# Another order of the opening, and other waits and stores in the last block, of a causal convolution with matrix taps

## Chip, cores and metric

The kernel runs on one core of a Trainium2 chip. The metric is the device time of one execution in microseconds (us); with several executions, the median. A profile of one execution shows what each engine did: PE (the matrix engine; PEld are its weight loads), DVE (vector), ACT (scalar), POOL (GpSimd) and SP, which here only issues transfers. TensorE's granted clock was 0.997 of full speed in the profiled execution.

## What is computed

```python
B, S, D, K = 8, 4096, 512, 8
for k in range(K):
    if k == 0:
        shifted = x
    else:
        shifted = np.concatenate([np.zeros((B, k, D)), x[:, :-k, :]], axis=1)
    out += np.matmul(shifted, kernel[k])
```

Each output row is a sum over eight taps: the row of x that lies k steps back, times a 512 x 512 matrix. x and the output are float32, 64 MiB each; the kernel multiplies in bf16 and adds in float32.

## The kernel before

**Tiling.** The 8 x 4096 rows are cut into 128 runs of 256 consecutive rows, and the 128 runs lie side by side: "row t" below is row t of all runs at once, a 128 x 512 tile. `XR` holds 20 such rows of x, transposed (channels on the partitions) and in bf16, as a ring; `place(t)` says where row t lies. A product (`product`, line 123) is four matmuls of 128 x 128 by 128 x 512 into one PSUM bank.

**The fast scheme.** Rows 0 to 3 (`HEAD`) are made directly, with 32 products (`direct`). The other 252 rows are made in 21 blocks of 12. A block has four nodes, PL, MI, H1 and H0, numbered 1 to 84. A node forms sums of rows on DVE (`node_z`, `node_A`, `node_s`, `node_F`, into the tiles `Z`, `S`, `F`), multiplies them with taps or with sums and differences of taps (the tiles W, made once by `wsum` and `plus` on DVE), nine products a node (eleven in the two leaf nodes, 3 and 4), and combines the results in PSUM and SBUF. So fewer products are needed than eight a row. The steps of a node, by the names in the order that is written out by hand: `a1`, `a0`, `u` (three products into a pair of banks `pp3`), `s0`, `s1` (ACT copies a seed from there into the banks of the lower and the upper output pair), `dt` (ACT copies the other bank to the tile `DT`), `v0`, `v1` (a product onto each seed), `d0`, `d1` (DVE makes the pair's other bank from it and `DT`), `l00` to `l11` (a product into each of the four banks), `e0`, `e1` (ACT or DVE takes each pair out to the tiles cc, dd, yy and stores it), `ga0` to `gb1` (`middle_half`, line 299: POOL adds the halves of the middle outputs of two tiles; when both halves are done SP stores the pair), and `ya0` (POOL subtracts one half of the lower output). The transposes `x12`, `x16`, `x20` bring the rows of the next block into `XR`, and `r0` to `r2` load rows three blocks ahead.

**What sets the order.** Nothing is scheduled by a planner: every engine works off its instructions in the order of the text, and waits on semaphores for its inputs. The opening (lines 430 to 643) is a list written out by hand; `go(k, name)` and `do(name, k)` in it run steps of the first nodes ahead of their block. From there `ORDER` (line 387) gives the sequence of a block, and `done` keeps what the opening has already run from running again. POOL issues all loads of x and of the taps (`load`, line 92), each of which turns float32 into bf16 on the way, and DRAM tiles (`xd`) hold rows of x until SP's transposes (`transpose`, line 98) move them to `XR`. SP issues the transposes and nearly all stores, one after the other. `behind` (line 111) makes a POOL instruction wait until the DVE operation issued last before it has ended. The tiles of outputs (`y`) are five, in turn.

**The last pair.** The last node is 84 (H0). Its upper output pair is written and stored by halves (lines 273 to 276), the lower half j = 0 on ACT's queue, then j = 1 on SP's. Both halves read the pair's banks in one tile (`pp1`), and the tile of dd that POOL reads in the last middle half, `ga1` of node 83.

Of the kernel before, what the change touches and what calls it, by code (L numbers as in the profile page):

```python
# [8 lines left out]
LO, HI, MID = 0, 1, 2  # L9
H1, H0, MI, PL = 0, 1, 2, 3  # L10
# [4 lines left out]
def kernel(  # L15
# [79 lines left out]
    def rows(o, t, n):  # L95
        return load(o, xr[:, t:t + n, :])
# [9 lines left out]
    def load_x(t):  # L106
        if t < RUN:
            xd[t] = dpool.tile([P, 4, D], bf, name="xd")
            return rows(xd[t], t, 4)

    def behind(i):
        tc.add_manual_dep(i.ins, last["dve"].ins.name,
                          mybir.DependencyInfo(mybir.DependencyClass.Sync, mybir.DependencyReason.DATA),
                          reason="behind")

    def transpose_x(t):
        if t < RUN:
            transpose(t, xd[t])
# [101 lines left out]
    def node_v(n, b_):  # L220
        if not n.leaf:
            product(n.p[b_][:, 1], comps(n)[2][1 + 2 * b_], W[n.a, b_, MID], False)

    def node_d(n, b_):
        if n.leaf:
            return
        p = n.p[b_]
        if b_ == LO:
            tt(p[:, 0], DT, p[:, 1], SUB)
        else:  # L230
            stt(p[:, 0], p[:, 1], -1.0, DT, SUB)
# [17 lines left out]
    def node_e(n, b_):  # L249
        p, t = n.p[b_], n.t + 2 * b_  # L250
        first = n.k <= 4
        if n.a == PL:
            cc[b_] = y_tile()
            if first:
                nc.scalar.mul(out=cc[b_], in_=p, mul=0.5)  # L255
            else:
                nc.scalar.copy(out=cc[b_], in_=p)  # L257
                dd[b_] = y_tile()
                nc.scalar.mul(out=dd[b_], in_=cc[b_], mul=-0.5)  # L259
        elif n.a == MI:  # L260
            if first:
                dd[b_] = y_tile()
                stt(dd[b_], p, -0.5, cc[b_], ADD)
            else:
                stt(dd[b_], p, 0.5, dd[b_], ADD)
        elif n.a == H1:
            yy[b_] = yy.get(b_) or y_tile()
            if first or b_ == HI:
                tt(yy[b_], p, dd[b_], ADD if first else SUB)
                store(t, yy.pop(b_))  # L270
            else:
                tt(yy[b_][:, 0], p[:, 0], dd[b_][:, 0], SUB)
        elif n.k == len(nodes) - 1 and b_ == HI:
            for j, eng in enumerate((nc.scalar, nc.sync)):
                stt(dd[b_][:, j], dd[b_][:, j], -1.0, p[:, j], SUB)
                eng.dma_start(out=orr[:, t + 8 + j, :], in_=dd[b_][:, j])
        else:
            if first:
                tt(dd[b_], dd[b_], p, SUB)
            else:  # L280
                stt(dd[b_], dd[b_], -1.0, p, SUB)
            store(t + 8, dd[b_])
# [14 lines left out]
        store(n.t + 4 + 2 * b_, cc[b_])  # L297

    def middle_half(n, b_, j):
        behind(nc.gpsimd.tensor_tensor(out=cc[b_][:, j], in0=cc[b_][:, j], in1=dd[b_][:, j], op=ADD))  # L300
        halves[b_] = halves.get(b_, 0) + 1
        if halves[b_] % 2 == 0:
            store(n.t + 4 + 2 * b_, cc[b_])

    halves = {}
# [1 line left out]
    def load_w(tap):  # L307
        n = K - 1 - tap
        load(W[n >> 2, n >> 1 & 1, n & 1], kr[:, :, tap, :])
# [10 lines left out]
    def wsum(a, b_, c_):  # L320
        p, m = terms(a, b_, c_)
        tt(W[a, b_, c_], p, m, SUB)
# [7 lines left out]
    def plus(*which):  # L330
        for b_, c_ in which:
            tt(W[PL, b_, c_], W[H0, b_, c_], W[H1, b_, c_], ADD)
# [7 lines left out]
    def transpose_pe(name, k, src, t0, t1):  # L340
        o = pair(k).bitcast(bf).rearrange("p a (b d) -> p (a b) d", b=2)
        for t in range(t0, t1):
            for c in range(DC):
                nc.tensor.transpose(o[:, t - t0, c * P:(c + 1) * P], src[:, t, c * P:(c + 1) * P],
                                    ident)
        bank[name] = o[:, 0:t1 - t0]
# [12 lines left out]
    def here(eng, t, name, a, b):  # L359
        eng(out=XR[:, place(t) + a:place(t) + b], in_=bank[name][:, a:b])  # L360

    def load_xin(t, a=0, b=4):
        rows(xin[t][:, a:b], t + a, b - a)
# [6 lines left out]
    def direct(tap, t):  # L370
        n = K - 1 - tap
        product(pd[t // 2][:, t % 2], XR[:, place(t - tap)], W[n >> 2, n >> 1 & 1, n & 1], tap == 0)
# [54 lines left out]
    def go(k, name):  # L427
        do("a1" if name == "b1" else name, k + AHEAD.get(name, 0))
# [30 lines left out]
    direct(1, 1)  # L459
    direct(1, 3)  # L460
    wsum(MI, HI, HI)
    direct(1, 0)
    load_w(5)
    plus((HI, HI))
    wsum(H1, HI, MID)
    direct(4, 1)
    load_w(3)
    plus((HI, LO))
    direct(5, 1)
    go(3, "d1")  # L470
    direct(4, 3)
    wsum(MI, HI, LO)
    direct(5, 3)
    wsum(H0, MID, LO)
    load_w(7)
    wsum(PL, HI, MID)
    direct(5, 2)
    wsum(MI, HI, MID)
    direct(3, 1)
    plus((LO, LO))  # L480
    wsum(PL, MID, LO)
    direct(3, 2)
    direct(3, 3)
    rows(H[:, 1:4], RUN - 7, 3)
    direct(7, 3)
    transpose_pe("h3", 2, H, 1, 4)
    direct(1, 2)
    load_w(6)
    wsum(MI, LO, LO)
    history(nc.scalar.copy, -7, "h3")  # L490
    direct(3, 0)
    wsum(H1, MID, LO)
    direct(7, 1)
    direct(6, 1)
    direct(7, 2)
    load_w(2)
    load_xin(4)
    load_xin(8, 0, 2)
    direct(6, 0)
    wsum(H1, MID, HI)  # L500
    go(3, "F0")
    wsum(H1, MID, MID)
    direct(7, 0)
    direct(5, 0)
    plus((LO, HI))
    wsum(PL, MID, HI)
    wsum(PL, LO, MID)
    go(2, "v1")
    wsum(MI, LO, HI)
    direct(2, 1)  # L510
    transpose_pe("x4", 3, xin[4], 0, 4)
    go(3, "d0")
    load_xin(8, 2, 4)
    direct(2, 0)
    here(nc.scalar.copy, 4, "x4", 2, 4)
    load_x(12)
    here(nc.scalar.copy, 4, "x4", 0, 2)
    transpose_x(12)
    wsum(PL, MID, MID)
    transpose_pe("x8", 2, xin[8], 0, 2)  # L520
    transpose_pe("x9", 2, xin[8], 2, 4)
    here(nc.scalar.copy, 8, "x8", 0, 2)
    wsum(MI, MID, HI)
    here(nc.scalar.copy, 10, "x9", 0, 2)
    load_x(16)
    fill(pair(3))
    z_rows(nodes[1], 0, 5)
    direct(6, 3)
    direct(2, 3)
    direct(6, 2)  # L530
    node_A(nodes[1])
    node_a1(nodes[1])
    direct(2, 2)
    go(3, "F1")
    z_rows(nodes[1], 5, 7)
    direct_out(0)
    s_rows(nodes[1], 0, 3)
    fill(pair(2))
    node_u(nodes[1])
    node_seed(nodes[1], 0)  # L540
    s_rows(nodes[1], 3, 5)
    node_seed(nodes[1], 1)
    node_a0(nodes[1])
    node_v(nodes[1], 0)
    node_dts(nodes[1])
    node_z(nodes[2])
    go(3, "v1")
    node_v(nodes[1], 1)
    node_F(nodes[1], 0)
    direct_out(1)  # L550
    node_A(nodes[2])
    wsum(MI, MID, LO)
    wsum(MI, MID, MID)
    node_d(nodes[1], 0)
    go(2, "v0")
    node_a1(nodes[2])
    for t in range(20, 52, 4):
        load_x(t)
    go(1, "l00")
    node_d(nodes[1], 1)  # L560
    go(1, "l01")
    go(1, "e0")
    go(1, "u")
    go(1, "F1")
    go(1, "s")
    go(1, "s0")
    go(1, "a0")
    go(1, "z")
    wsum(MI, LO, MID)
    go(1, "l11")  # L570
    go(1, "s1")
    go(1, "v1")
    go(4, "F1")
    go(1, "A")
    go(1, "l10")
    go(1, "dt")
    go(1, "e1")
    go(1, "d1")
    go(1, "a1")
    go(1, "v0")  # L580
    go(1, "F0")
    go(2, "a0")
    wsum(H1, LO, MID)
    go(1, "d0")
    go(2, "F1")
    go(2, "u")
    go(2, "l00")
    go(2, "s")
    wsum(H0, MID, HI)
    go(2, "l10")  # L590
    go(2, "l01")
    go(2, "s0")
    go(2, "e0")
    go(2, "dt")
    wsum(H0, MID, MID)
    go(2, "s1")
    go(2, "l11")
    go(2, "z")
    go(3, "s")
    go(2, "A")  # L600
    go(3, "l01")
    go(3, "l10")
    do("x12", 1)
    do("x16", 1)
    go(2, "e1")
    go(3, "g0")
    go(3, "dt")
    go(2, "a1")
    go(3, "z")
    go(3, "l00")  # L610
    go(3, "a0")
    go(3, "u")
    go(3, "l11")
    go(2, "d0")
    go(3, "e0")
    go(3, "A")
    go(3, "e1")
    go(3, "s0")
    do("x20", 1)
    go(2, "F0")  # L620
    go(4, "l01")
    go(4, "l00")
    go(3, "s1")
    go(4, "b1")
    go(4, "s")
    go(4, "F0")
    go(4, "l11")
    go(4, "a0")
    go(4, "e0")
    go(4, "u")  # L630
    go(4, "l10")
    go(4, "dt")
    go(4, "s1")
    go(4, "z")
    go(4, "A")
    go(4, "g1")
    go(4, "s0")
    go(4, "v0")
    go(4, "d0")
    go(4, "v1")  # L640
    go(4, "e1")
    go(4, "a1")
    go(4, "d1")

    done |= {(name, k) for name in ("ga0", "gb0", "ga1", "gb1", "x12", "x16", "x20")
# [41 lines left out]
```

## Time and profile before

| | |
|---|---|
| median of 3 runs (lowest to highest) | 719.75 us (719.42 to 720.0) |
| the profiled execution | 720.38 us, its span 718.6 us |
| granted clock of TensorE in it | 0.997 |
| bytes moved, mean rate | 138.87 MB by the queues, 193 GB/s |

Busy time by stretch of the profiled execution (us):

| stretch | PE | DVE | ACT | POOL |
|---|---|---|---|---|
| 0 to 10 | 7.05 | 1.16 | 4.25 | 6.67 |
| 10 to 20 | 8.50 | 2.53 | 1.85 | 2.45 |
| 20 to 30 | 10.00 | 9.67 | 0.54 | 2.14 |
| 30 to 40 | 9.57 | 9.54 | 2.27 | 2.57 |
| 40 to 50 | 7.27 | 9.93 | 5.05 | 1.03 |
| 50 to 60 | 9.26 | 9.43 | 4.67 | 0 |
| 60 to 100 | 39.83 | 38.20 | 14.92 | 0 |
| 100 to 700 | 597.45 | 595.05 | 251.37 | 147.73 |
| 700 to 710 | 10.00 | 7.51 | 2.69 | 3.81 |
| 710 to 718.6 | 0.40 | 1.29 | 0 | 1.26 |

How to read it: an engine that is busy for the whole of a stretch bounds it, one that has idle time there waits for another, and the view of idle times says for which. Matmuls overlap in the pipeline, so PE's busy time says when it had work, and the distance from one matmul's start to the next one's says how fast it went. In the lines of a timeline, the columns are the start, the time, the engine, the source line, the operation with its output and inputs, and in brackets the idle time before it with what ended it. All lines `L84` and `L87` are the helpers `tt` and `stt`, so the operations are told apart by their tiles.

### The profile page before, as it was taken

The page shows a single profiled execution, that of the slowest core. Times are in us where ns is not written, and L with a number is a line of the kernel's source. Part 1 is how long each engine was busy: PE and PEld are TensorE (multiplying, and loading weights), DVE is VectorE, ACT ScalarE, POOL GpSimd, SP SyncE. Part 2 cuts the span into 40 slices and gives each one's busy share as a digit, 9 for nine tenths or more (in the row PEclk, how much of TensorE's full clock was granted, in tenths as well). Part 3 has the DMA queues.
Part 4 walks back from the last instruction along what each step waited for, and adds up shares of the span by engine and source line. Part 5 has one row for each costly group of instructions (what it writes and reads, how often), then busy time and mean ns, then how long its engine had stood idle before and what let it go on. Part 6 is the DMA issues. An engine that isn't in the chain of part 4 may idle for free.

```text
span 718.6 us, 9022 instructions
## 1 busy us (share of the span) xinstructions
PE 699.3 (97%) x3270; PEld 314.9 (44%) x3270; DVE 684.3 (95%) x767; ACT 287.6 (40%) x448; POOL 167.6 (23%) x180
## 2 busy tenths in 40 slices
PE   7989999999999999999999999999999999999995
PEld 3444444444444444444444444444444444444442
DVE  2899999999999999999999999999999999999994
ACT  3043244443534434352443434354443435344341
POOL 4210013223041221304122130412213131221212
PEclk9999999999999999999999999999999999999998
DMA  9999559697797868868787887978787687756414
GB/s 193 209 212 226 181 119 257 147 234 179 206 211 183 247 155 231 185 190 205 192 247 151 236 179 208 220 179 235 165 237 173 205 224 177 225 127 192 150 59 176
DMA packets 159372, 138.87 MB, mean 193 GB/s; under 512 B 130144, under 2 KB 134240, under 8 KB 159200
## 3 DMA queue, kind: packets, MB, share of 16 engines
q1 hardware_dynamic: 145456, 99.89, 45.6%
q0 software_dynamic: 13728, 38.15, 31.2%
q8 instruction: 25, 0.41, 0.2%
q10 hardware_dynamic: 144, 0.26, 0.1%
q14 instruction: 19, 0.16, 0.1%
HBM read 77.33 MB, written 99.09 MB: 246 GB/s over the span
## 4 chain that ended last, share of the span: by engine, by line
PE 79%; DVE 10%; issue 2%; DMA 1%; POOL 1%; ACT 0%; POOLq 0%; DVEq 0%
PE pp L125 79%; DVE Z L84 4%; DVE S L84 1%; DVE y L87 1%; DMA out_dram<-y 1%; DVE F L84 1%; DVE w L84 1%; POOL y L300 1%; DVE y L84 1%; DVE pp L84 0%; DVE pp L87 0%; POOLq L682 0%; POOL xd L93 0%; ACT y L255 0%; ACT pp L212 0%
## 5 line engine op out<-in xcount | busy, mean ns | idle before, releaser
L125 PE MATMUL pp<-w,F 128*128 128x512 bf16 x1312 | 312.9, 379 | 1.0 <-DVE pp L87 0.7
L125 PE MATMUL pp<-w,Z 128*128 128x512 bf16 x960 | 233.9, 379 | 1.7 <-DVE Z L84 1.6
L300 POOL TENSOR_TENSOR y<-y 128x512 f32<-128x512 f32 x80 | 101.7, 1271 | 445.4 <-DVE F L84 327.7
L125 PEld LDWEIGHTS <-F 128*128 128x128 bf16 x1312 | 128.3, 98 | 156.6 <-issue 2.4
L125 PE MATMUL pp<-w,S 128*128 128x512 bf16 x672 | 158.8, 379 | 0.0
L84 DVE TENSOR_TENSOR Z<-XR 128x2048 bf16<-128x2048 bf16 (+3 forms) x109 | 154.7, 1438 | 2.4
L125 PEld LDWEIGHTS <-Z 128*128 128x128 bf16 x960 | 92.2, 98 | 118.7 <-DVE Z L84 10.3
L196 ACT COPY pp<-pp 128x512 f32<-128x512 f32 x82 | 46.7, 570 | 221.7 <-PE pp L125 221.7
L84 DVE TENSOR_TENSOR S<-Z 128x2560 bf16<-128x2560 bf16 (+1 forms) x81 | 114.7, 1416 | 0.0
L84 DVE TENSOR_TENSOR F<-S 128x1024 bf16<-128x1024 bf16 x160 | 111.4, 696 | 1.9 <-PE pp L125 1.9
L125 PEld LDWEIGHTS <-S 128*128 128x128 bf16 x672 | 65.7, 98 | 79.3
L212 ACT COPY pp<-pp 128x512 f32<-128x512 f32 (+1 forms) x84 | 48.8, 581 | 74.9 <-PE pp L125 74.9
L84 DVE TENSOR_TENSOR pp<-DT,pp 128x512 f32<-128x512 f32 x82 | 56.6, 690 | 1.3 <-PE pp L125 1.2
L87 DVE SCALAR_TENSOR_TENSOR pp<-pp,DT 128x512 f32<-128x512 f32 x82 | 56.8, 693 | 0.5 <-PE pp L125 0.5
L214 ACT ACTIVATE pp<-pp 128x512 f32<-128x512 f32 (+1 forms) x84 | 50.1, 597 | 14.3 <-PE pp L125 8.1
L84 DVE TENSOR_TENSOR Z<-Z 128x1024 bf16<-128x1024 bf16 x78 | 53.5, 686 | 0.7
L87 DVE SCALAR_TENSOR_TENSOR y<-pp,y 128x1024 f32<-128x1024 f32 x42 | 51.2, 1218 | 0.5 <-PE pp L125 0.5
L218 ACT COPY DT<-pp 128x512 f32<-128x512 f32 x82 | 48.9, 597 | 3.9 <-PE pp L125 3.9
L87 DVE SCALAR_TENSOR_TENSOR y<-y,pp 128x1024 f32<-128x1024 f32 (+1 forms) x41 | 48.4, 1184 | 1.7 <-POOL y L300 1.4
L257 ACT COPY y<-pp 128x1024 f32<-128x1024 f32 x40 | 40.7, 1016 | 22.9 <-PE pp L125 22.9
L93 POOL DMA_DIRECT2D xd<-in_x_dram x61 | 32.8, 537 | 65.2 <-DVE F L84 48.5
L259 ACT ACTIVATE y<-y 128x1024 f32<-128x1024 f32 x40 | 42.3, 1057 | 2.5 <-DMA out_dram<-y 0.4
(35 smaller groups left out, 248.9 us busy)
## 6 DMA issues: line engine op xcount, KB each, us to landing
out_dram<-y SPq DMA_DIRECT2D x127, 512.0 KB, 4.1
xd<-in_x_dram POOLq DMA_DIRECT2D x61, 512.0 KB, 5.3
w<-in_kernel_dram POOLq DMA_DIRECT2D x8, 512.0 KB, 17.0
w<-in_x_dram SPq DMA_DIRECT2D x1, 1024.0 KB, 4.8
w<-in_x_dram POOLq DMA_DIRECT2D x2, 512.0 KB, 13.7
XR<-xd SPq DMA_TRANSPOSE x61, 4.7
w<-in_x_dram POOLq DMA_DIRECT2D x2, 256.0 KB, 17.4
w<-in_x_dram POOLq DMA_DIRECT2D x1, 384.0 KB, 20.4
```

The costliest lines, as they stand in the source:

```text
L84: last["dve"] = nc.vector.tensor_tensor(out=o, in0=a, in1=b, op=op)
L87: last["dve"] = nc.vector.scalar_tensor_tensor(out=o, in0=a, scalar=by, in1=b, op0=MUL, op1=op)
L93: return nc.gpsimd.dma_start(out=o, in_=src)
L125: nc.tensor.matmul(bank, lhsT=comp[:, c * P:(c + 1) * P], rhs=w[:, c, :], start=start and c == 0, stop=c == DC - 1, skip_group_check=True)
L196: nc.scalar.copy(out=n.q[:, 0], in_=n.q[:, 1])
L212: nc.scalar.copy(out=o, in_=q)
L214: nc.scalar.mul(out=o, in_=q, mul=-1.0)
L218: nc.scalar.copy(out=DT, in_=n.q[:, 0])
L257: nc.scalar.copy(out=cc[b_], in_=p)
L259: nc.scalar.mul(out=dd[b_], in_=cc[b_], mul=-0.5)
L300: behind(nc.gpsimd.tensor_tensor(out=cc[b_][:, j], in0=cc[b_][:, j], in1=dd[b_][:, j], op=ADD))
```

## The change

Five things change; the products, sums and loads are the same ones as before.

1. The list of the opening from line 462 on stands in another order: the weight sums, the products of the direct rows, the PE transposes of rows 4 to 11 and the steps of nodes 1 to 8. `wsum(H1, HI, MID)`, `wsum(H1, MID, HI)` and `wsum(H1, MID, MID)` move back among the steps of the nodes; the transposes of rows 12 (`transpose_x(12)`) and 20 (`do("x16", 1)`) move behind the two direct outputs, the one of rows 16 (`do("x12", 1)`) behind that of rows 20.
2. The loads of rows 40, 44 and 48 move to the end of the opening's list, in the order 48, 40, 44, and wait for the DVE operation before them (`behind`).
3. In the last block, POOL's last half (`ga1` of node 83) is not held behind a DVE operation.
4. The two banks of the last node's upper pair lie in two tiles: the lower one moves to `pp3`, and node 84's `d1` writes it there.
5. The last middle output is stored by halves on ACT's queue, each when its half is done. The halves of the last upper pair are taken in the order upper, lower; the upper one is stored on ACT's queue and the lower one on SP's.

```diff
-    def behind(i):
+    def behind(i, k=0):
+        if k > len(nodes) - 5:
+            return
         tc.add_manual_dep(i.ins, last["dve"].ins.name,
...
+    class Apart:
+        def __init__(self, lo, hi):
+            self.banks = lo, hi
+
+        def __getitem__(self, i):
+            return self.banks[i[1]][:, i[1]]
+
     def node_d(n, b_):
         if n.leaf:
             return
+        if n.k == len(nodes) - 1 and b_ == HI:
+            n.p[b_] = Apart(pair(3), n.p[b_])
         p = n.p[b_]
...
         elif n.k == len(nodes) - 1 and b_ == HI:
-            for j, eng in enumerate((nc.scalar, nc.sync)):
+            for j, eng in ((HI, nc.scalar), (LO, nc.sync)):
                 stt(dd[b_][:, j], dd[b_][:, j], -1.0, p[:, j], SUB)
                 eng.dma_start(out=orr[:, t + 8 + j, :], in_=dd[b_][:, j])
...
     def middle_half(n, b_, j):
-        behind(nc.gpsimd.tensor_tensor(out=cc[b_][:, j], in0=cc[b_][:, j], in1=dd[b_][:, j], op=ADD))
+        behind(nc.gpsimd.tensor_tensor(out=cc[b_][:, j], in0=cc[b_][:, j], in1=dd[b_][:, j], op=ADD), b_ > j and n.k)
         halves[b_] = halves.get(b_, 0) + 1
-        if halves[b_] % 2 == 0:
+        if b_ and n.k > len(nodes) - 5:
+            nc.scalar.dma_start(out=orr[:, n.t + 6 + j, :], in_=cc[b_][:, j])
+        elif halves[b_] % 2 == 0:
             store(n.t + 4 + 2 * b_, cc[b_])
```

Of the opening's list, the new order of the parts that the prediction speaks of, with the rest left out:

```python
    wsum(MI, HI, HI)
    load_w(5)
    load_w(3)
    wsum(MI, HI, LO)
...
    plus((HI, LO))
    wsum(MI, HI, MID)
    go(3, "F1")
    plus((HI, HI))
    plus((LO, LO))
    wsum(PL, HI, MID)
...
    z_rows(nodes[1], 0, 5)
    node_A(nodes[1])
    load_x(12)
    transpose_pe("x9", 2, xin[8], 2, 4)
...
    for t in range(20, 40, 4):
        load_x(t)
...
    direct_out(1)
    go(1, "l01")
    go(1, "l00")
    node_d(nodes[1], 1)
    go(1, "e0")
    go(1, "u")
    go(1, "a0")
    transpose_x(12)
    go(1, "l10")
    go(1, "z")
    do("x16", 1)
...
    go(2, "e1")
    behind(load_x(48))
    go(3, "s")
...
    go(4, "l00")
    behind(load_x(40))
    go(4, "b1")
    go(4, "l10")
    behind(load_x(44))
```

More of the change, by code (lines that the diff above doesn't have):

```diff
@@ L461 @@
     wsum(MI, HI, HI)
+    load_w(5)
+    load_w(3)
+    wsum(MI, HI, LO)
     direct(1, 0)
-    load_w(5)
-    plus((HI, HI))
-    wsum(H1, HI, MID)
-    direct(4, 1)
-    load_w(3)
-    plus((HI, LO))
+    load_w(7)
+    direct(5, 3)
+    plus((HI, LO))
+    wsum(MI, HI, MID)
+    go(3, "F1")
+    plus((HI, HI))
+    plus((LO, LO))
+    wsum(PL, HI, MID)
+    rows(H[:, 1:4], RUN - 7, 3)
+    load_w(6)
+    direct(1, 2)
+    direct(4, 1)
+    wsum(H1, MID, LO)
+    direct(3, 0)
+    direct(4, 3)
@@ L469 @@
+    direct(3, 3)
+    load_w(2)
+    load_xin(4)
     direct(5, 1)
[L470 to L473, printed above, removed]
+    direct(3, 1)
     wsum(H0, MID, LO)
[L475 to L480, printed above, removed]
     wsum(PL, MID, LO)
-    direct(3, 2)
-    direct(3, 3)
-    rows(H[:, 1:4], RUN - 7, 3)
+    transpose_pe("h3", 2, H, 1, 4)
+    load_xin(8, 0, 2)
+    go(4, "F1")
     direct(7, 3)
-    transpose_pe("h3", 2, H, 1, 4)
@@ L487 @@
-    direct(1, 2)
-    load_w(6)
     wsum(MI, LO, LO)
     history(nc.scalar.copy, -7, "h3")
[L491 to L502, printed above, removed]
+    direct(6, 3)
+    wsum(H0, MID, HI)
+    plus((LO, HI))
+    direct(3, 2)
+    direct(6, 2)
+    direct(5, 2)
+    direct(5, 0)
+    direct(2, 1)
+    wsum(MI, LO, HI)
+    transpose_pe("x4", 3, xin[4], 0, 4)
@@ L503 @@
+    wsum(PL, MID, HI)
+    transpose_pe("x8", 2, xin[8], 0, 2)
     direct(7, 0)
-    direct(5, 0)
-    plus((LO, HI))
-    wsum(PL, MID, HI)
+    here(nc.scalar.copy, 4, "x4", 0, 2)
+    wsum(MI, LO, MID)
     wsum(PL, LO, MID)
[L508 to L512, printed above, removed]
+    wsum(MI, MID, HI)
     load_xin(8, 2, 4)
     direct(2, 0)
+    here(nc.scalar.copy, 8, "x8", 0, 2)
+    go(3, "d1")
+    wsum(PL, MID, MID)
+    direct(7, 1)
@@ L515 @@
     here(nc.scalar.copy, 4, "x4", 2, 4)
[L516 to L525, printed above, removed]
     fill(pair(3))
     z_rows(nodes[1], 0, 5)
-    direct(6, 3)
+    node_A(nodes[1])
+    load_x(12)
+    transpose_pe("x9", 2, xin[8], 2, 4)
     direct(2, 3)
-    direct(6, 2)
@@ L531 @@
-    node_A(nodes[1])
+    here(nc.scalar.copy, 10, "x9", 0, 2)
+    s_rows(nodes[1], 0, 3)
+    direct(6, 0)
+    z_rows(nodes[1], 5, 7)
     node_a1(nodes[1])
[L533 to L537, printed above, removed]
+    load_x(16)
+    wsum(H1, MID, HI)
+    s_rows(nodes[1], 3, 5)
+    direct(6, 1)
+    go(2, "v1")
     fill(pair(2))
     node_u(nodes[1])
+    node_z(nodes[2])
+    node_a0(nodes[1])
+    go(1, "F1")
+    node_A(nodes[2])
+    direct_out(0)
@@ L540 @@
+    node_dts(nodes[1])
+    direct(7, 2)
     node_seed(nodes[1], 0)
-    s_rows(nodes[1], 3, 5)
     node_seed(nodes[1], 1)
-    node_a0(nodes[1])
-    node_v(nodes[1], 0)
-    node_dts(nodes[1])
-    node_z(nodes[2])
-    go(3, "v1")
+    wsum(MI, MID, LO)
+    node_F(nodes[1], 0)
+    for t in range(20, 40, 4):
+        load_x(t)
+    direct(2, 2)
+    node_v(nodes[1], 0)
+    node_d(nodes[1], 0)
+    go(2, "F0")
+    wsum(MI, MID, MID)
+    node_a1(nodes[2])
+    go(1, "s")
     node_v(nodes[1], 1)
-    node_F(nodes[1], 0)
@@ L550 @@
     direct_out(1)
[L551 to L558, printed above, removed]
+    go(1, "l01")
     go(1, "l00")
     node_d(nodes[1], 1)
-    go(1, "l01")
     go(1, "e0")
     go(1, "u")
-    go(1, "F1")
-    go(1, "s")
-    go(1, "s0")
     go(1, "a0")
+    transpose_x(12)
+    go(1, "l10")
     go(1, "z")
-    wsum(MI, LO, MID)
+    do("x16", 1)
     go(1, "l11")
     go(1, "s1")
+    wsum(H1, MID, MID)
@@ L572 @@
+    go(1, "s0")
+    go(1, "v0")
+    go(1, "dt")
+    go(1, "F0")
+    go(1, "A")
+    go(1, "d0")
+    go(1, "a1")
+    go(2, "F1")
     go(1, "v1")
[L573 to L576, printed above, removed]
+    go(2, "l01")
+    go(2, "l00")
+    go(2, "a0")
+    go(2, "u")
     go(1, "e1")
     go(1, "d1")
[L579 to L589, printed above, removed]
@@ L590 @@
-    go(2, "l10")
-    go(2, "l01")
     go(2, "s0")
-    go(2, "e0")
     go(2, "dt")
     wsum(H0, MID, MID)
-    go(2, "s1")
+    go(3, "dt")
+    go(2, "s")
+    go(3, "v1")
+    go(2, "e0")
     go(2, "l11")
     go(2, "z")
-    go(3, "s")
+    do("x12", 1)
+    go(2, "l10")
+    go(3, "l00")
+    go(2, "s1")
+    go(2, "a1")
     go(2, "A")
     go(3, "l01")
-    go(3, "l10")
[L603 to L613, printed above, removed]
-    go(2, "d0")
[L615 to L620, printed above, removed]
+    go(3, "u")
+    go(2, "e1")
+    behind(load_x(48))
+    go(3, "s")
+    go(3, "z")
+    go(3, "l11")
+    go(3, "g0")
+    go(4, "g1")
+    wsum(H1, LO, MID)
+    go(3, "a0")
+    wsum(H1, HI, MID)
+    go(2, "v0")
+    go(3, "F0")
+    do("x20", 1)
+    go(3, "e0")
+    go(3, "s0")
+    go(3, "A")
+    go(3, "l10")
@@ L621 @@
+    go(3, "e1")
+    go(2, "d0")
     go(4, "l01")
+    go(3, "s1")
     go(4, "l00")
-    go(3, "s1")
+    behind(load_x(40))
     go(4, "b1")
+    go(4, "l10")
+    behind(load_x(44))
     go(4, "s")
+    go(4, "u")
+    go(4, "e0")
+    go(4, "s1")
+    go(4, "s0")
+    go(4, "l11")
+    go(4, "z")
     go(4, "F0")
-    go(4, "l11")
+    go(4, "A")
     go(4, "a0")
-    go(4, "e0")
-    go(4, "u")
-    go(4, "l10")
     go(4, "dt")
[L633 to L636, printed above, removed]
@@ L637 @@
-    go(4, "s0")
+    go(3, "d0")
+    go(4, "e1")
     go(4, "v0")
+    go(4, "v1")
+    go(4, "a1")
     go(4, "d0")
-    go(4, "v1")
-    go(4, "e1")
-    go(4, "a1")
     go(4, "d1")
```

## The prediction

> **What bounds the kernel now.** I read the page first (shares of the span), then a table of stretches, then the idle times of DVE and PE in the opening, and last the timeline, the issues and the DMA rate of the final 18 us.
>
> ```profile
> PE 699.3 (97%) x3270; PEld 314.9 (44%) x3270; DVE 684.3 (95%) x767; ACT 287.6 (40%) x448; POOL 167.6 (23%) x180
> ...
> 200.00:300.00 100.00, 100.00 (x464) 45.00 (x463) 99.14 (x112) 41.53 (x67) 26.05 (x27) 1.00 0.80 201
> ```
>
> The reader is to see two full engines: from 200 to 300 us PE is busy 100.00 of 100.00 us and DVE 99.14. A block of four nodes is 36 products of four matmuls, and the timeline has eight matmuls in 1.725 us (101.84 less 100.12), so PE needs 31.1 us a block; DVE has under 1% to spare beside it. Whatever the opening loses on either engine is therefore never caught up, and whatever it saves reaches the end. Only the opening and the last 10 us can be worth anything.
>
> ```profile
> 20.24 4.63 DVE L84 TENSOR_TENSOR w<-w,w 128x2048 bf16<-128x2048 bf16 x4 [2.62 <-DMA w<-in_kernel_dram]
> ...
> 31.07 1.40 DVE L84 TENSOR_TENSOR w<-w,w 128x2048 bf16<-128x2048 bf16 x1 [0.34 <-issue]
> ...
> 59.21 0.70 DVE L87 SCALAR_TENSOR_TENSOR pp<-pp,DT 128x512 f32<-128x512 f32 x1 [0.50 <-PE pp L125]
> ...
> 66.08 1.23 DVE L87 SCALAR_TENSOR_TENSOR y<-pp,y 128x1024 f32<-128x1024 f32 x1 [0.52 <-PE pp L125]
> ...
> 86.94 0.69 DVE L84 TENSOR_TENSOR pp<-DT,pp 128x512 f32<-128x512 f32 x1 [0.98 <-PE pp L125]
> ```
>
> These are DVE's waits in the opening, from the first weight sum (15.26) on: one for a tap's landing, one around the history copy, three for PE. The matmul rows show PE waiting in its turn: 1.62 us at 41.52, 1.21 at 49.38, 0.74 at 56.33.
>
> **The opening, reordered.** The two orders, read beside each other on DVE: from its first weight sum, 124 operations end at the same operation, and in both they are the same operations by shape and number; only their order differs. So their working time is the same, and I compare what lies between them. Back to back, the next one starts 0.08 us before the last ends (21.38 after a 20.24 start of 1.22); after an operation whose result it reads, it starts 0.035 us later (43.29 after 41.77 plus 1.48), so each such pair costs 0.12 us.
> Before: waits of 2.62, 0.55 (31.28 is where the cleared history row starts, 0.55 after DVE's last end), 0.50, 0.52 and 0.98, together 5.17 us; 17 short gaps, together 0.83; 22 lost overlaps of 0.08, 1.8. Sum 7.8 us.
> After, laid out with the durations of these rows (an operation starts when its engine is free and its last input is there, loads landing as before): one weight sum now stands ahead of the landing at 20.24 where two stood, so the wait grows to 20.24 - 16.48 = 3.76; four sums of 1.135 us later the next wanted pair, taps 3 and 7, lands at 25.32: 0.49. The clearing of the history row now comes at 32.1, when ACT's copy has been done for two us: nothing. The three waits for PE go: PE does the products that DVE wants first (the two seeds' products 0.4 to 0.7 us ahead near 60 us, the first outputs 1.2 to 1.7 us ahead at 64 to 67). The thinnest is at 86.5 us, where product and DVE meet within 0.02 us; if PE is late there, DVE loses that much. Nine dependent pairs remain, 0.3 us, and 11 lost overlaps, 0.9. Sum 5.5 us, so 2.3 us are saved. Laid out in the same way, the order of before brings DVE to its 125th operation at 141.9 us where the trace has 142.13; against that the saving is 2.0. I take 2.1.
> PE agrees: its gaps after 15 us (0.5, 1.8, 1.3, 0.9 and some 1.8 in small ones up to 120) become 0.5, 0.2, 1.95 (at 41.4, for node 1's sums), 0.6, 0.2 and 0.7. That is about 2 us as well. Bounds: 2.3 above; below, if the thin places slip by half a us each and the extra waits at two semaphores (0.09 instead of 0.035 us) show in all pairs, 0.7.
>
> **Loads and transposes.** The loads of rows 40, 44 and 48 leave the opening's queue and are tied to DVE operations near 68, 79 and 80 us. Cost nothing: their transposes come at 126 us and later, a steady load takes 5.3 us, so 40 us cover them; POOL has nothing else before 104.5 us. The software queue then ends with rows 36, whose load lands at 55.4 instead of 63.4 us. Rows 12's transpose is issued behind the two direct stores, at 53.0 instead of 39.81:
>
> ```profile
> 39.81 20.49 SPq L100 DMA_TRANSPOSE XR<-xd  x1
> 60.36 1.21 SPq L242 DMA_DIRECT2D out_dram<-y  x2
> 61.67 7.21 SPq L100 DMA_TRANSPOSE XR<-xd  x2
> ```
>
> Before, it held SP for 20.49 us beside the loads, landed only at 64.5 when those were through, and the two stores stood behind it. After, loads run beside it for 2.4 us, so I let it land near 58, and rows 20 and 16 at 62 and 64. DVE wants rows 12 to 15 at 65.1 and rows 16 to 23 at 69.5: cover of 7 and 5 us. The stores go at 46.6 and 52.6; nobody waits for them.
>
> **The last block.** On the clock of before:
>
> ```profile
> 706.78 3.62 PE L125 MATMUL pp<-w,F 128*128 128x512 bf16 x16
> ...
> 707.93 1.27 POOL L300 TENSOR_TENSOR y<-y 128x512 f32<-128x512 f32 x1 [0.65 <-DVE y L84]
> 708.78 1.22 DVE L87 SCALAR_TENSOR_TENSOR y<-y,pp 128x1024 f32<-128x1024 f32 x1 [0.32 <-PE pp L125]
> 710.08 1.26 POOL L300 TENSOR_TENSOR y<-y 128x512 f32<-128x512 f32 x1 [0.88 <-DVE y L87]
> 711.37 1.29 DVE L87 SCALAR_TENSOR_TENSOR y<-y,pp 128x512 f32<-128x512 f32 x2 [1.38 <-POOL y L300]
> ```
>
> POOL's last half, no longer tied to the DVE operation, starts at 709.20 and ends at 710.47. DVE's upper half needs only its own bank (done four matmuls before PE's end at 710.40, so 709.54) and POOL's earlier half (709.20): 709.92 to 710.61. The lower half needs PE's end and POOL's 710.47: 710.53 to 711.21, where the second half ended at 712.66. DVE ends 1.45 us sooner; the middle output, now in two halves, costs ACT's queue two issues of 0.37 us where SP had one of 0.33. The new tile costs nothing: its bank was last read by ACT at 704.39 to 704.99, 2.8 us before DVE writes it. POOL beside DVE's output operation is nothing new: 707.93 to 709.20 against 708.78 to 710.00, both at their usual 1.27 and 1.22. The issue moved to ACT's queue finds ACT idle since 705.
>
> But what ends the kernel is the last store:
>
> ```profile
> GB/s 143 410 410 389 430 389 410 369 471 389 410 348 451 225 307 369 451 389 410 389 307 430 389 430 369 430 410 287 410 369 389 389 358 410 174 0 0 0 0 0
> ...
> q1 hardware_dynamic: 720, 2.36, 74.3%
> q10 hardware_dynamic: 144, 0.26, 8.6%
> ```
>
> This is the DMA rate from 708 to 716 us in slices of 0.2 us: from 708.1 to 714.9 the engines write at about 390 GB/s with one dent, near 710.7. Four stores and two half-stores stand in line, and those before hold back the last one. 2.62 MB at the 400 GB/s of the undented slices take 6.55 us, so from 708.15 they cannot end before 714.7, against 714.9. The change sends the same bytes after the same start (the first of these stores, issued at 707.32, doesn't move); a half that is ready 1.35 us sooner fills the dent. Worth 0.2 us, not 1.45. Bounds: 0, if the 2 KB packets of two queues mix badly; 1.45, if two queues at once move more than one. Queue q10, alone for about 0.7 us, ran at the same rate as q1, so I stay at the low end.
>
> The Trainium skill, "DMA: Bandwidth & Descriptors", section "Anatomy of one DMA", gives a DMA a fixed 2.0 us plus its bytes at 436 GB/s: an estimate of 2.6 us for a half-store, and the trace has 2.7 for the last. By that rule alone the last store would land 1.45 us sooner and the sum would be 716.2; the rate row says that the engines are full, and I go by the row. The same page's "Issuing engines are not separate DMA queues" speaks against a gain from the second queue as such.
>
> **Sum.** 2.1 + 0.2 = 2.3 us. The profiled execution took 720.38 us (span 718.6, 1.8 around it), 0.6 over the median of the runs; from it, 718.1, and from the median 719.75, 717.5.
>
> **Rivals.**
> A: two queues move more than one, or the stores' own 2.7 us from issue decide. Then the tail is worth 1.45 and the time is 719.75 - 2.1 - 1.45 = 716.2. For it: every late store took 2.6 to 2.7 us, as in quieter stretches. Against it: the full rate row.
> B: the opening gives back what it saves. DVE gives up 1.1 us of work in the cover of the first landings and must do it later; if PE is late at 86.5 us and at the first outputs by what it was late before (0.98 and 0.52 us), 0.6 is left, and with the tail 719.0. For it: both engines are full and the margins thin.
> C, slower: the transpose of rows 12 starves behind the loads as before. If it takes the 24.7 us that it took from issue to landing, it lands at 77.7 instead of 58; DVE, in order, stands from 65.1 for 12.6 us, and the time is 719.75 - 2.3 + 12.6 = 730. It decides from a landing past 65.1. For it: the one row above. Against it: the queue that starved it ends 8 us sooner, and the next two transposes took 7.2 us together.
> D: the last half of POOL is still held, by its place behind the other half: only the order of the halves acts, and since stores bound the end nothing changes but 0.1 us.
>
> **Chances.** Forecast (717.0 to 718.3) 0.55, A 0.14, B (and D with it) 0.24, C 0.07. The range runs from A's 716.2 to 719.2, which takes in most of B and leaves out C and little more. A measurement of this kernel can tell about 0.2%, 1.44 us, from no change: faster (below 718.3) 0.70, same 0.23, slower 0.07.
>
> **What would show it.** Right: DVE's wait before 20.24 near 3.8 us, none for PE between 25 and 120; the steady pattern about 2 us sooner; rows 12's transpose landed before 62; DVE's end 3.5 us sooner, the DMA rate without a dent, the last landing some 4.7 us after PE's end instead of 5. Wrong: a wait of DVE for a transpose, a new wait of PE at 60 to 100 us, or a DMA rate over 450 GB/s while both queues store.

## The result and the profile after

| | before | after |
|---|---|---|
| median (lowest to highest), 12 runs each | 719.97 us (718.77 to 721.04) | 717.89 us (716.43 to 718.95) |
| ratio, 95% interval | | 0.9975 (0.9966 to 0.9984) |
| the profiled execution, its span | 720.38 us, 718.6 | 718.95 us, 717.2 |
| granted clock in it | 0.997 | 0.998 |

The ratio stands for 1.8 us (1.2 to 2.4); 717.5 had been predicted. The total is as forecast, but its two terms are not: the opening gave half of what was expected of it, and the last block more, for a reason that the prediction did not have.

The busy times on the page of after, and the stretch from 200 to 300 us by the table of stretches (PE, PEld, DVE, ACT and POOL busy, instructions in brackets, then clock, DMA share and GB/s):

```profile
PE 696.0 (97%) x3205; PEld 315.0 (44%) x3270; DVE 683.3 (95%) x767; ACT 287.7 (40%) x448; POOL 167.5 (23%) x180
```

```profile
200.00:300.00 100.00, 99.53 (x454) 45.02 (x462) 97.72 (x111) 42.11 (x68) 26.36 (x28) 1.00 0.80 202
```

65 matmul records are missing (3205 of 3270 weight loads), so PE's sums can't be compared; DVE's 767 are all there. DVE's 97.72 holds one wait of 1.59 us near 300 us, for a store that still read the tile to be written. Before had the same wait with 1.53 us, just after the stretch; a second near 550 us took 1.40 against 0.51. Such waits are in all traces and change between executions.

DVE's opening in after, by the timeline (the lines with a wait, and those of its thin places):

```profile
14.87 1.23 DVE L84 TENSOR_TENSOR w<-w,w 128x2048 bf16<-128x2048 bf16 x1 [1.77 <-DMA w<-in_kernel_dram]
19.95 4.63 DVE L84 TENSOR_TENSOR w<-w,w 128x2048 bf16<-128x2048 bf16 x4 [3.86 <-DMA w<-in_kernel_dram]
25.79 1.23 DVE L84 TENSOR_TENSOR w<-w,w 128x2048 bf16<-128x2048 bf16 x1 [1.21 <-DMA w<-in_kernel_dram]
...
32.97 0.14 DVE L370 MEMSET XR<- 128x96 bf16 x1
34.08 2.34 DVE L84 TENSOR_TENSOR w<-w,w 128x2048 bf16<-128x2048 bf16 x2
...
86.50 0.69 DVE L84 TENSOR_TENSOR pp<-DT,pp 128x512 f32<-128x512 f32 x1
```

The first wait grew to 3.86 us as laid out (3.76), and the three waits for PE are gone; the thin place at 86.50 held. But a second wait for a landing, laid out at 0.49, took 1.21 us. From the first weight sum to the 125th operation DVE took 125.77 us, where before took 126.87: 1.1 us saved.

SP's queue in after, where the transpose of rows 12 had been the danger:

```profile
47.26 6.49 SPq L253 DMA_DIRECT2D out_dram<-y  x2
53.87 8.77 SPq L100 DMA_TRANSPOSE XR<-xd  x3
```

Three transposes go out in 8.77 us, where one had held the queue for 20.49. By their records they landed at 60.03, 62.94 and 65.08 us; DVE took up the first at 65.83 and, for rows 16 to 23, the other two at 70.22, without a wait.

The last block in after, by the timeline, and the DMA rate from 708 to 716 us in slices of 0.2 us with the two queues:

```profile
706.24 3.62 PE L127 MATMUL pp<-w,F 128*128 128x512 bf16 x15
...
707.40 2.51 POOL L311 TENSOR_TENSOR y<-y 128x512 f32<-128x512 f32 x2 [0.65 <-DVE y L84]
708.24 2.42 DVE L87 SCALAR_TENSOR_TENSOR y<-y,pp 128x1024 f32<-128x1024 f32 x3 [0.31 <-PE pp L127]
708.70 1.57 ACTq L314 DMA_DIRECT2D out_dram<-y  x2
710.31 1.19 ACTq L287 DMA_DIRECT2D out_dram<-y  x1
710.69 0.33 SPq L287 DMA_DIRECT2D out_dram<-y  x1
```

```profile
GB/s 389 369 471 389 410 369 471 369 369 389 369 389 369 420 420 410 451 389 379 389 379 348 348 430 348 399 420 338 379 420 348 113 0 0 0 0 0 0 0 0
...
q1 hardware_dynamic: 534, 1.66, 53.1%
q10 hardware_dynamic: 432, 0.79, 26.2%
```

POOL's two halves run back to back and DVE's output follows in one row of 2.42 us. The dent is filled, the mean of the slices is still about 390 GB/s, and the last store landed at 714.72 us. That is 5.45 us after PE's last weight load; before it was 5.56. So 0.1 us came of the stores, about as predicted. Yet the end of the span came 7.90 us after that weight load, where before took 8.81: 0.9 us less. A landing that moved by 0.1 can't account for that. The balance of the two spans: first sum 0.39 earlier, opening 1.10, tail 0.91, less 0.95 for DVE's two waits near 300 and 550 us, gives 1.45, the difference of 718.62 and 717.17.

### The profile page after: what moved, and what is told of

Read it like the earlier page. It is cut to its first block, busy times and chain, and to the rows that moved or that the text cites. A ratio compares the mean times of both kernels' runs of the same rounds, so it can differ in the third digit from the quotient of the medians.

```text
span 717.2 us, 8960 instructions
## 1 busy us (share of the span) xinstructions
PE 696.0 (97%) x3205; PEld 315.0 (44%) x3270; DVE 683.3 (95%) x767; ACT 287.7 (40%) x448; POOL 167.5 (23%) x180
## 4 chain that ended last, share of the span: by engine, by line
PE 84%; DVE 5%; issue 5%; DMA 0%; POOL 0%; DVEq 0%; POOLq 0%
PE pp L127 84%; DVE w L84 2%; DVE Z L84 2%; DVE y L87 1%; DVE S L84 1%; DMA out_dram<-y 0%; POOL y L311 0%; DVE y L84 0%; DVE F L84 0%; DVE pp L87 0%; DVE pp L84 0%; POOL xd L93 0%; DVEq L84 0%; DVEq L87 0%; POOLq L93 0%
## 5 line engine op out<-in xcount | busy, mean ns | idle before, releaser
L127 PEld LDWEIGHTS <-S 128*128 128x128 bf16 x672 | 65.8, 98 | 79.4 <-issue 0.2
```

The source lines that it names most:

```text
L127: nc.tensor.matmul(bank, lhsT=comp[:, c * P:(c + 1) * P], rhs=w[:, c, :], start=start and c == 0, stop=c == DC - 1, skip_group_check=True)
```

## The experiments

All eight were timed against before, five rounds each and three for the last. "After PE" counts from PE's last weight load, since matmul records can be missing; "opening" is DVE's time from its first weight sum to its 125th operation. The median is over all executions, the last four columns are of the one that was profiled. All times in us.

| kernel | median | ratio to before (95%) | opening | POOL's last operation ends, after PE | last landing, after PE | end of span, after PE |
|---|---|---|---|---|---|---|
| before | 719.97 | | 126.87 | 1.53 | 5.56 | 8.81 |
| after | 717.89 | 0.9975 (0.9966 to 0.9984) | 125.77 | 0.64 | 5.45 | 7.90 |
| e1_opening | 718.92 | 0.9988 (0.9979 to 0.9997) | 125.88 | 1.53 | 5.57 | 8.80 |
| e2_last | 718.46 | 0.9984 (0.9975 to 0.9993) | 126.89 | 0.63 | 5.48 | 7.89 |
| e7_free | 717.89 | 0.9974 (0.9965 to 0.9983) | 126.39 | 0.63 | 4.92 | 7.90 |
| e8_swap | 717.29 | 0.9966 (0.9954 to 0.9979) | 124.58 | 0.63 | 5.47 | 7.90 |
| e12_untie | 719.14 | 0.9987 (0.9978 to 0.9996) | 126.89 | 0.62 | 5.56 | 7.89 |
| e9_pooloff | 715.65 | 0.9930 (0.9916 to 0.9944) | 126.96 | -4.38 | 4.20 | 5.61 |
| e10_both | 714.63 | 0.9919 (0.9906 to 0.9933) | 124.93 | -4.39 | 4.19 | 5.59 |
| e5_loads | 721.43 | 1.0019 (1.0007 to 1.0032) | 129.63 | 0.62 | 5.45 | 7.83 |

### e1_opening: the opening alone

The opening of after (parts 1 and 2), with the last block of before; against after, with the lines on the tile `Apart` left out:

```diff
-    def behind(i, k=0):
-        if k > len(nodes) - 5:
-            return
+    def behind(i):
...
-            for j, eng in ((HI, nc.scalar), (LO, nc.sync)):
+            for j, eng in enumerate((nc.scalar, nc.sync)):
...
-        if b_ and n.k > len(nodes) - 5:
-            nc.scalar.dma_start(out=orr[:, n.t + 6 + j, :], in_=cc[b_][:, j])
-        elif halves[b_] % 2 == 0:
+        if halves[b_] % 2 == 0:
```

> The new opening (order, loads, transposes) with the last block as before. If the opening carries the gain and the stores bound the end: 1.4 to 2.1 us under before, ratio 0.997 to 0.998, the steady pattern as early as in the changed kernel, and from the last matmul's start to the last landing 5.35 us as before. If the last block carried it: under 0.6 us, ratio above 0.999.

Measured: 0.9 us (0.2 to 1.5) faster than before, and 1.0 us less on DVE in the opening, with the tail as in before to 0.01 us. That is less than the 1.4 to 2.1 us expected if the opening carries the gain. So the opening is worth about 1 us, not 2.1.

### e2_last: the last block alone

The opening of before, with parts 3 to 5; against after, the first lines of the opening's list that differ:

```diff
+    direct(1, 0)
     load_w(5)
+    plus((HI, HI))
+    wsum(H1, HI, MID)
...
-    direct(1, 0)
-    load_w(7)
```

> The opening of before with the new last block. If the write rate bounds the end: DVE ends 1.4 to 1.5 us sooner after the last matmul than before (1.2 instead of 2.6 us), but the last landing comes only 0.1 to 0.2 us sooner (5.15 to 5.25 us after the last matmul's start instead of 5.35), and the time is 0.1 to 0.3 us under before, which the runs cannot tell from nothing (ratio 0.9995 to 1.000). If the stores' time from issue decides: 1.45 us under before, ratio 0.998.

Measured: 1.15 us (0.5 to 1.8) faster, against a landing only 0.08 us earlier after PE. The theory that the write rate of the stores decides the end could give 0.1 to 0.3 and falls; that each store's own time decides falls with it, since the landing hardly moved. Something else ends the execution.

SP's waits name it indirectly. First before, then e2_last (engine and line, what was waited for, sum, times, longest); line 682 and line 695 are the kernel's end:

```profile
SPq L682 <- PEq L682: 2.9, 2, 2.4
SPq L682 <- DMA out_dram<-y: 1.9, 2, 1.3
```

```profile
SPq L695 <- DMA out_dram<-y: 3.2, 2, 2.0
SPq L695 <- PEq L695: 2.1, 2, 1.6
```

After the last store had landed SP stood in the closing barrier for another 2.4 us in before, and 1.6 in e2_last: it had the stores behind it and waited for a partner. The engine named there is only the one whose semaphore came last. The records at the end of each trace, which these views leave out, show the partner (times from the span's start):

```
                               before    e12_untie  after     e9_pooloff
POOL  last TENSOR_TENSOR ends  711.339   709.961    709.905   703.986
POOL  closing DRAIN ends       717.474   716.096    716.039   710.119
      difference                 6.135     6.135      6.134     6.133
SP    done with last store     715.58    715.10     714.93    712.77
      end of the span          718.62    717.23     717.17    713.97
```

In each of the ten traces POOL's closing drain ends 6.13 us after its last tensor operation, and in eight of them it is the last thing before the closing barrier, with the span's end 1.08 to 1.14 us after it. Only where POOL is done early (e9_pooloff and e10_both) do the stores come last: 1.41 us from the last landing, at 712.56 in e9_pooloff, to the end. The new theory: POOL's last operation sets the end, 7.3 us behind it (6.13 + 1.1). In after that operation ends 0.89 us sooner after PE than in before, and the tail is 0.91 shorter. The next three sections bear on it: e7_free was set up together with the first two, before this theory, e12_untie and e9_pooloff to test it.

### e7_free: stores sooner, POOL's last operation not

after, with the last subtraction of POOL (`ya0` of node 83) not held behind DVE either:

```diff
-            behind(nc.gpsimd.tensor_tensor(out=y[:, 1], in0=y[:, 1], in1=dd[LO][:, 1], op=SUB))
+            behind(nc.gpsimd.tensor_tensor(out=y[:, 1], in0=y[:, 1], in1=dd[LO][:, 1], op=SUB), n.k)
```

> The changed kernel, and in the last block POOL's subtracted half is not held behind DVE either, so that its 512 KB store goes out some 3 us or more sooner, while the transfers idle; no issue after it moves. If the write rate bounds the end: the last landing comes 0.6 to 0.8 us sooner after the last matmul's start than in the changed kernel (4.5 instead of 5.24 us), the time 0.6 to 0.8 us under the changed kernel's. If the stores' time from issue, or DVE's end, decides: no change, 5.2 us.

POOL in e7_free, by the timeline:

```profile
701.10 1.27 POOL L303 TENSOR_TENSOR y<-y 128x512 f32<-128x512 f32 x1 [0.60 <-ACT y L298]
...
705.81 2.50 POOL L311 TENSOR_TENSOR y<-y 128x512 f32<-128x512 f32 x2 [3.45 <-DVE y L84]
```

The subtraction moved forward, its store with it, and the last landing came 0.53 us sooner after PE (4.92 against 5.45). The end did not move (7.90), nor did the median (717.89 in both). A landing half a microsecond earlier is worth nothing here.

### e12_untie: part 3 alone

before, with one dependency less:

```diff
-        behind(nc.gpsimd.tensor_tensor(out=cc[b_][:, j], in0=cc[b_][:, j], in1=dd[b_][:, j], op=ADD))
+        behind(nc.gpsimd.tensor_tensor(out=cc[b_][:, j], in0=cc[b_][:, j], in1=dd[b_][:, j], op=ADD), b_ > j and n.k)
```

> The kernel before, with one part of the change alone: POOL's last half in the last block is not held. If the end hangs on POOL (its closing drain ended 6.13 us after its last operation in each trace so far, and the execution 1.14 us later): POOL's last operation ends 0.9 us sooner after PE's last weight load (0.64 instead of 1.53 us) and so does the execution (7.9 instead of 8.8 us); 0.9 us under before, ratio 0.9985 to 0.999. If the last store's landing decides: 0.1 us at most.

POOL's two halves in e12_untie, and DVE's and the queues' last lines:

```profile
707.47 2.49 POOL L302 TENSOR_TENSOR y<-y 128x512 f32<-128x512 f32 x2 [0.65 <-DVE y L84]
...
710.03 1.28 DVE L87 SCALAR_TENSOR_TENSOR y<-y,pp 128x512 f32<-128x512 f32 x2 [0.50 <-POOL y L302]
710.75 0.37 ACTq L278 DMA_DIRECT2D out_dram<-y  x1
711.34 0.33 SPq L278 DMA_DIRECT2D out_dram<-y  x1
```

DVE's end and the landing are later than in after (1.97 against 1.39, and 5.56 against 5.45), yet the span ends 7.89 us after PE as there, and the median is 0.9 us (0.3 to 1.6) under before. So the untied half makes the gain of the last block by itself. Parts 4 and 5 bring 0.6 us on DVE and 0.1 on the landing, none of which reaches the end.

### e9_pooloff: POOL's last operations taken away

after, with the last two middle halves as one DVE operation, 5 us earlier in DVE's order, and one store on SP's queue:

```diff
     def middle_half(n, b_, j):
-        behind(nc.gpsimd.tensor_tensor(out=cc[b_][:, j], in0=cc[b_][:, j], in1=dd[b_][:, j], op=ADD), b_ > j and n.k)
+        if b_ and n.k > len(nodes) - 5:
+            if j:
+                tt(cc[b_], cc[b_], dd[b_], ADD)
+                store(n.t + 6, cc[b_])
+            return
+        behind(nc.gpsimd.tensor_tensor(out=cc[b_][:, j], in0=cc[b_][:, j], in1=dd[b_][:, j], op=ADD))
         halves[b_] = halves.get(b_, 0) + 1
-        if b_ and n.k > len(nodes) - 5:
-            nc.scalar.dma_start(out=orr[:, n.t + 6 + j, :], in_=cc[b_][:, j])
-        elif halves[b_] % 2 == 0:
+        if halves[b_] % 2 == 0:
...
-    LATE = {(0, "F1.4"): [("wl", 8)], (1, "s.2"): [("wh", 8)]}
+    LATE = {(0, "F1.4"): [("wl", 8)], (1, "s.2"): [("wh", 8)], (NB - 1, "s1.3"): [("gb1", len(nodes) - 2)]}
```

It also has e7_free's edit.

> The changed kernel, and in the last block POOL's two middle halves are one DVE operation of 1.22 us in DVE's idle 1.93 us before the last F, stored whole by SP at once, and POOL's subtracted half is not held. If the end hangs on POOL's drain until something else is later: the drain ends some 0.5 us after PE's last weight load, long before the last landing (near 4.0 us after it, since the stores are spread and nothing queues), and the execution ends 5.4 us after PE's last weight load instead of 7.9: 2.5 us under the changed kernel. If the write rate decided: 0.5 to 1.4 us under it, by the landing alone.

The wait of DVE in after that takes in the moved operation:

```profile
704.56 0.69 DVE L84 TENSOR_TENSOR F<-S 128x1024 bf16<-128x1024 bf16 x1 [1.93 <-PE pp L127]
```

The moved operation in e9_pooloff, POOL's last one beside it, what is left of that wait, and the output:

```profile
701.65 1.21 DVE L84 TENSOR_TENSOR y<-y 128x1024 f32<-128x1024 f32 x1
...
701.78 2.21 POOL L303 TENSOR_TENSOR y<-y 128x512 f32<-128x512 f32 x1 [0.60 <-ACT y L298]
703.66 0.88 DVE L84 TENSOR_TENSOR F<-S 128x1024 bf16<-128x1024 bf16 x1 [0.80 <-PE pp L127]
...
707.32 2.41 DVE L87 SCALAR_TENSOR_TENSOR y<-y,pp 128x1024 f32<-128x1024 f32 x3 [0.30 <-issue]
```

The end moved to 5.61 us after PE, 2.3 sooner than in after, and the median to 715.65. The added 1.21 us lie in a wait of DVE for PE: 1.93 us before 704.56 in after, of which 0.80 is left before 703.66 in e9_pooloff. So they cost the path next to nothing: DVE's last operation ends 1.37 us after PE's last weight load, 1.39 in after. The drain now ends 2.44 us before the last landing, so here the stores do set the end; that is where the prediction's bound would have held.

The opening of this execution, 126.96 us, is no shorter than that of before, though it has after's order. Its trace shows one thing that no other has: the granted clock is 0.50 from 44.0 to 47.4 us, right behind PE's wait of 2.12 us, and in that stretch the matmuls start 0.427 us apart instead of 0.216, 1.7 us lost on PE. In after, e1_opening, e7_free and e5_loads the same wait (2.10 to 2.11) left the clock at 1.00. How often it happens in executions that were not profiled is not known.

### e8_swap: work put back into the cover of the landings

after, with sums that the new order had taken out from under the first landings put back, and two others exchanged:

```diff
     wsum(MI, HI, HI)
+    plus((HI, HI))
     load_w(5)
...
     wsum(MI, HI, MID)
+    wsum(H1, HI, MID)
+    wsum(PL, HI, MID)
     go(3, "F1")
-    plus((HI, HI))
     plus((LO, LO))
-    wsum(PL, HI, MID)
...
-    wsum(H0, MID, HI)
+    wsum(H1, MID, HI)
...
-    wsum(H1, MID, HI)
+    wsum(H0, MID, HI)
...
-    wsum(H1, HI, MID)
```

> The changed kernel with DVE's waits for the first taps filled: plus(HI, HI) goes ahead of the wait at 20 us, wsum(H1, HI, MID) and wsum(PL, HI, MID) ahead of the one at 25.8, and wsum(H1, MID, HI) changes places with wsum(H0, MID, HI). If DVE's order bounds the opening: the waits shrink from 3.86 and 1.21 to 2.7 and nothing, node 1's sums come 0.7 to 1.1 us sooner, DVE waits some 1 us for PE at 83 to 87 us instead, and the time is 0.7 to 1.0 us under the changed kernel's. If PE alone bounds it by 86 us: no change.

DVE's waits in e8_swap's opening:

```profile
13.95 2.36 DVE L84 TENSOR_TENSOR w<-w,w 128x2048 bf16<-128x2048 bf16 x2 [0.66 <-DMA w<-in_kernel_dram]
19.03 4.63 DVE L84 TENSOR_TENSOR w<-w,w 128x2048 bf16<-128x2048 bf16 x4 [2.72 <-DMA w<-in_kernel_dram]
...
82.56 1.22 DVE L84 TENSOR_TENSOR y<-y,pp 128x1024 f32<-128x1024 f32 x1 [0.36 <-PE pp L127]
84.29 0.70 DVE L84 TENSOR_TENSOR pp<-DT,pp 128x512 f32<-128x512 f32 x1 [0.51 <-PE pp L127]
```

The wait for the first landing shrank from 3.86 to 2.72 us and the second one is all but gone; 0.87 us of waits for PE came back at 82 to 84 us. DVE's opening took 124.58 us, 1.2 less than in after, and the median is 0.6 us lower; its interval overlaps that of after.

### e10_both

e8_swap's opening with e9_pooloff's last block.

> e9_pooloff with the opening of e8_swap. If the two places add up: 0.7 to 1.2 us under e9_pooloff, 3 to 3.7 us under the changed kernel, ratio to before 0.991 to 0.993. If a new bound shows, the sum falls short.

714.63 us, 0.81% (0.67 to 0.94) under before, and 1.0 under e9_pooloff by the medians, as expected if the two places add up. How much of that 1.0 is e9_pooloff's stretch at half the clock is open. It is the fastest of these kernels.

### e5_loads: without part 2

after, with the loads of rows 40, 44 and 48 in the opening's queue again:

```diff
-    for t in range(20, 40, 4):
+    for t in range(20, 52, 4):
...
-    behind(load_x(48))
...
-    behind(load_x(40))
...
-    behind(load_x(44))
```

> The changed kernel with rows 40, 44 and 48 loaded in the opening's queue again, ahead of the transposes. If the transposes starve beside loads: rows 12's transpose lands near 64.5 us and rows 20's and 16's near 69 and 71, close to where DVE wants them (65.8 and 70.2): 0 to 1 us lost, a wait of DVE for a transpose at 66 to 71. If they do not starve: no wait, no change. Rival C's 12 us would need a landing at 78.

The expectation was far off. SP's transposes in e5_loads, then DVE's waits for them:

```profile
53.26 16.51 SPq L100 DMA_TRANSPOSE XR<-xd  x3
```

```profile
67.65 1.22 DVE L84 TENSOR_TENSOR Z<-XR 128x2048 bf16<-128x2048 bf16 x1 [2.35 <-DMA XR<-xd]
...
73.01 2.09 DVE L84 TENSOR_TENSOR Z<-XR 128x1536 bf16<-128x1536 bf16 x2 [0.88 <-DMA XR<-xd]
```

Beside loads that landed up to 65.8 us, three transposes held SP for 16.51 us instead of 8.77, and DVE waited 3.23 us for two of them. The time is 3.5 us over that of after, slower than before even: the new order needs part 2.

## Why the prediction was right in sum and wrong in its terms

**The opening, "the next wanted pair, taps 3 and 7, lands at 25.32: 0.49" (term 2.1, measured 1.1).** The mechanism was right: the work is the same, DVE's idle time alone changed, and the three waits for PE vanished as laid out. The step that failed is a landing time read from one execution. In the five traces with the new order DVE's second wait was 1.21, 1.31, 1.59, 1.58 and 1.75 us, never 0.49. In after's records tap 7 lands 5.84 us after tap 5, where before's trace has 5.1. The packets of one load go to 16 engines; in nine of the ten traces one of the 16 parts landed 0.6 to 1.3 us after the fifteenth, in each load from the sixth to the fourteenth; in before's profiled execution alone it was mostly 0.03 to 0.07. The order of before does not feel it: e2_last had 0.74 to 0.79 of it in the loads of taps 3 and 7, e12_untie 1.05 to 1.08, and both took 126.89 us. The new order, with less work in front of that landing, does. In after this makes 0.7 of the missing 1.0 us; the history row's clearing, put at nothing, cost 0.28 (it starts 0.28 after DVE's last end), and the first wait 0.1 more. That the price lies at the landings, and not at PE, the traces of e8_swap and e10_both show: with the work back in front of them the opening takes 124.58 and 124.93 us, 1.2 and 0.8 less than in after (the gain of e8_swap's median, 0.6 us, is not clear of noise). By the runs the opening is worth 0.9 us (0.2 to 1.5). Single executions differ: with the same order the opening took 126.39 us in e7_free, where the two landings came later still, and 126.96 in e9_pooloff.

**PE's gaps, "about 2 us as well" (measured 0.9).** Laid out: 0.5, 0.2, 1.95, 0.6, 0.2, 0.7. Measured as waits: 0.24 at 23.25, 0.83 at 30.11, 2.10 at 44.28, 0.43 at 53.09, 0.33 at 118.89. The large one is there, and nothing from 60 to 100 us. But the second was laid out at 0.2. The weight loads, of which no record is missing, give the sum: from 15 to 130 us, what lies between two of them beyond the steady 0.216 us adds up to 6.98 us in before and 6.09 in after (distances over 0.33 us counted).

**Loads and transposes, at nothing.** Right: rows 12 landed at 60.03 (58 predicted), the next two at 62.94 and 65.08 (62 and 64), with 5.8 and 5.1 us to spare.

**The last block, "what ends the kernel is the last store" (term 0.2, measured 0.9).** DVE's end came 1.46 us sooner after PE (1.45 predicted), the dent was filled, and the landing moved 0.1: each step up to the landing held. The last one failed. The views end with the last busy instruction and the last transfer, and I took the later of these for the end, though the span of before ran on for 3.24 us behind it. In those 3 us POOL's drain ended. Undoing the tie alone gives the whole 0.9 us (e12_untie), an earlier landing nothing (e7_free), an earlier end of POOL 2.3 (e9_pooloff).

The two errors, 1.0 too much and 0.7 too little, nearly cancel: that the total came out is luck.

**The rivals.** A, a tail worth 1.45 by a second queue: the rate with both queues at work stayed where it was (mean of the slices 392 GB/s, before 388; single slices reach 451 and 471 in both), and the landing moved 0.1. Nor did the stores' own 2.7 us decide: the last four took 3.4 to 4.4 us from issue to landing. So its mechanism is refuted; that the tail gained more than 0.2 had another cause. The Trainium skill, "DMA: Bandwidth & Descriptors", section "Issuing engines are not separate DMA queues", says that issuing DMAs on several engines at once saves only the time it takes to initiate them, and the rate row agrees. The fit of 2.0 us plus bytes, which the prediction set against the rate row, stands in its section for DMAs that GpSimd issues, while SP and ACT issue these stores; the sum did not rest on it. B, the opening gives back: about half was given back. B's premise held, work taken out of the cover of the first landings, but the loss came at a landing, and not by PE being late at 86.5 us and at the first outputs. C, a starved transpose: not in after, but e5_loads shows the mechanism at 3.5 us (medians), where C had priced it at 12. D, POOL's half still held: refuted by the row of POOL's two halves back to back.

## What to carry to other kernels

Subtract the last landing from the end of the span before saying that the stores end a kernel; if there are some us left, ask for each engine when its closing instruction ended, and try ending GpSimd's work earlier. A landing time from one trace is a sample: an order that takes work out from under a landing must be priced with that landing late by what other loads show. A pair of edits can depend on one another: the reordered opening loses unless its later loads move too.

## What the runs showed of the hardware

- POOL's closing drain ended 6.13 us after POOL's last tensor operation in ten traces of ten (6.133 to 6.135), with the operation as late as 712.21 us or as early as 702.83. The operation was an addition or a subtraction of 128x512 float32 elements in all of them. Why it takes so long, and whether another kind of operation changes it, was not tried.
- Moved beside a DVE addition of two SBUF tiles (701.65 to 702.86), POOL's subtraction took 2.21 us, in e10_both as well; in e7_free, with no such operation beside it, 1.27. The Trainium skill, "SBUF — State Buffer", section "Who interferes with whom", says that a DVE instruction with two SBUF inputs contends with a GpSimd instruction that reads SBUF; the 0.94 us more agree.
- The DMA engines' rate stayed near 390 GB/s with one queue or two (388 in before, 392 in after).
- In e9_pooloff the granted clock fell to 0.50 for 3.4 us after a wait of PE of 2.12 us; four traces with the same wait kept it at 1.0.
- What remains open: why one of the 16 parts of the weight loads trails, and why not in before's profiled execution; why the clock fell in one trace only; the first weight sum itself starts anywhere from 13.5 to 15.3 us.
